# A hybrid decoder layer: turned blocks in a ring of five, and low parts of the gate/up operands on VectorE

## The chip, the cores and the metric

The kernel runs on one core of a Trainium2 chip. The core has a matrix engine (TensorE; PE in the profile, PEld for its weight loads), VectorE (DVE), ScalarE (ACT), GpSimd (POOL), SyncE (SP, which here only issues transfers), and 16 DMA engines. Each engine runs its own instructions in one fixed order and waits on semaphores for the others. The metric is the device time of one execution in microseconds; of several runs the median counts.

## The reference

One decoder layer on x of 2048 rows by 1024 columns, all float32:

```python
hn = rms_norm(h, mix_pre_g)
proj = hn @ w_in
attn_out = sliding_window_attention(q, k, v, attn_sinks, rel_bias)
conv_out = conformer_conv(u, conv_dw, conv_dw_b, conv_ln_g, conv_ln_b, w_conv_pw)
mixed = jnp.concatenate([attn_out, conv_out], axis=-1) @ w_out
h = h + rms_norm(mixed, mix_post_g)
hn = rms_norm(h, ffn_pre_g)
ff = (jax.nn.silu(hn @ w_gate) * (hn @ w_up)) @ w_down
h = h + rms_norm(ff, ffn_post_g)
```

The feed-forward width is 2816. The change touches the operands of `hn @ w_gate` and `hn @ w_up`.

## The kernel before

**Tiles.** The 2048 rows are four token tiles of 512 (`T`), numbered 0 to 3. A block is 128 partitions (`P`) by 512 columns, or 128 by 128 inside a transpose.

**High and low parts.** Every large float32 product is made of three faster ones. An operand x is split into a high part, which ScalarE writes by a copy into the reduced type float32r, and a low part, x minus the high part, which VectorE or GpSimd makes by a subtraction. `three` and `product` then add high by high, high by low and low by high into one PSUM bank. `split_f` makes the high part, `lo(x, w, on_pool)` the low part: on GpSimd if `on_pool` is true, otherwise on VectorE.

**Stages.** The letter before the @ of a label, or after it in the profile's names, tells the stage: A the input projection, B attention, C the convolution, J a join of two weight matrices, W the output projection with its norm, H the operands of gate and up, F gate and up, G the down projection and the last norm.

**Gate and up.** Stages H, F and G work on token tiles in pairs, first (0, 1), then (2, 3); `ws` holds the pair, so `ws[0]` is 0 or 2. Over a pair, gate and up are computed by a two-by-two block scheme with seven products instead of eight (`STEPS`); the weight blocks are A11 to A22 and their sums S1 to S4, the token blocks B11 to B22 and their sums T1 to T4. One product (`product`) is four blocks of 128 times three matmuls, 12 matmuls with 512 columns.

- `stage_h_plain` makes B11 or B21, the plain operands from the first tile of the pair: per block it loads columns of the normed rows, turns them on PE (`turned`) into a PSUM bank, copies them to a buffer `u` with the gain as scale, issues on ScalarE's queue a transfer that stores `u` in `hT`, and makes high and low part. For the first pair the turned blocks use the bank tag `ct`, of which there is one, and `u` the tag `gb`, of which there are two. The four blocks of B11 and the four of B21 make eight such copies. They run in the lane `lh` beside the output projection of tile 1 (`stage_w(1, ...)`), whose operands are named hl@W; attention on tile 3 runs there too.
- `stage_h_sums` makes T1 to T4 and B22, four blocks each; for T1, T3 and T4 the low part is made by GpSimd, for T2 by VectorE. It uses three tiles of tag `chl` per block, one of them for two blocks of `hT` read back.
- `stage_pre` runs the products of the first m with plain operands alone (A11 with B11, then A12 with B21), while the sums are made: 20 values of m in the first pair, 16 in the second, two products each. Its `split` makes the operands of the weights three products ahead. In the second pair the low parts of the odd ones, 16 in all, go to GpSimd.
- `stage_p1` runs the other products of the scheme. In the second pair it has GpSimd make some low parts of its own (`POOL_LO`) and the sums of finished blocks.

When the second pair's `stage_pre` runs, the last rows of the first pair's down projection are normed and stored beside it (`finish`, lane `lf`; names x@G, p@G, sm@G).

**Rings.** `t_(tag, ...)` takes the next buffer of a tag; `BUFS` says how many there are (`gb` 2, `chl` 5). A new tile waits until the tile that held the buffer last has been read for the last time, by a transfer too. A `chl` tile is two blocks wide.

**Order.** Lanes (`Lane`) are generators that are pumped as the main loop goes on, so the text order interleaves the stages. The framework then plans the order on each engine from that text order as a priority and its own estimate of times (`schedule_with_timeline_sim=True`), so that an instruction may be put ahead of others that were written before it.

Of the kernel before, what the change touches and what calls it, by code (L numbers as in the profile page):

```python
# [25 lines left out]
P = 128  # L26
T = 512
# [10 lines left out]
def layer_kernel(ctx, tc, x, xT, cols, rows, sinks, relb, onehot, w_in, w_pw, w_out, w_gate, w_up, w_down, out):  # L38
# [10 lines left out]
    def nm(s):  # L49
        uid[0] += 1  # L50
        return f"{s}@{lab[0]}_{uid[0]}"
# [3 lines left out]
    def t_(tag, shape, dt=F32):  # L55
        return sb.tile(list(shape), dt, tag=tag, name=nm(tag), bufs=BUFS[tag])
# [4 lines left out]
    def f2(tag, shape=(P, T)):  # L61
        return t_(tag, shape)

    def hl(tag):
        return t_(tag, (P, 2, T), F32R)
# [779 lines left out]
    def split_f(x, w):  # L845
        act(w[:, 0], x, AF.Copy)  # L846
        return w

    def lo(x, w, on_pool):
        (ptt if on_pool else vtt)(w[:, 1], x, w[:, 0].bitcast(F32), ALU.subtract)  # L850
# [9 lines left out]
    def turned(w, k, bank_of, tag):  # L860
        c = load_cols(w, k, tag)
        b = bank_of()
        for s in range(4):
            nc.tensor.transpose(b[:, s * P : (s + 1) * P], c[:, s], ident)
        return b

    def op_tile(ws, ops, n, k, spare):
        tag = OPTAG[ws[0]][n][k]
        if tag == "yt":
            if "yt" not in spare:  # L870
                spare["yt"] = t_("yt", (P, 2, 2, T), F32R)
            w = spare["yt"][:, k]
        else:
            w = hl(tag)
        ops.setdefault(n, []).append(w)
        return w

    def stage_h_plain(ws, ops, n, off):
        L = f"H{ws[0]}"
        for k in range(4):  # L880
            lab[0] = L
            b = turned(ws[0], k + off, tr if ws[0] else ct, COLTAG[ws[0]][k] if ws[0] else "fa")
            u = f2("gb")
            act(u, b, AF.Copy, scale=g_ffn[:, k + off : k + off + 1])
            nc.scalar.dma_start(hT[ws[0] // 2][k + off], u)
            o = op_tile(ws, ops, n, k, {})
            act(o[:, 0], u, AF.Copy)
            lo(u, o, False)
            yield 2.0

    def stage_h_sums(ws, ops):
        L = f"H{ws[0]}"
        spare = {}
        for k in range(4):
            lab[0] = L
            ct_ = COLTAG[ws[0]]
            g1, g2 = g_ffn[:, k : k + 1], g_ffn[:, k + 4 : k + 5]
            own = t_("chl", (P, 2, T))
            nc.sync.dma_start(own, hT[ws[0] // 2][k :: 4].rearrange("j p t -> p j t"))
            own = own[:, 0], own[:, 1]  # L900
            b12 = turned(ws[1], k, tr, ct_[2])
            b22 = turned(ws[1], k + 4, tr, ct_[3])
            r = t_("chl", (P, 2, T))
            t = t_("chl", (P, 2, T))
            act(r[:, 1], b12, AF.Copy, scale=g1)
            b = op_tile(ws, ops, "B22", k, spare)
            act(b[:, 0], b22, AF.Copy, scale=g2)
            yield 1.5
            lab[0] = L
            stt(r[:, 0], b12, g1, own[0], ALU.mult, ALU.subtract)  # L910
            stt(t[:, 0], b22, g2, r[:, 0], ALU.mult, ALU.subtract)
            stt(r[:, 1], b22, g2, r[:, 1], ALU.mult, ALU.subtract)
            stt(b[:, 1], b22, g2, b[:, 0].bitcast(F32), ALU.mult, ALU.subtract)
            vtt(t[:, 1], own[1], t[:, 0], ALU.subtract)
            yield 3
            for n, x in (("T1", r[:, 0]), ("T2", t[:, 0]), ("T3", r[:, 1]), ("T4", t[:, 1])):
                lab[0] = L
                o = op_tile(ws, ops, n, k, spare)
                act(o[:, 0], x, AF.Copy)
                lo(x, o, n != "T2")  # L920
                yield 0.8

    STEPS = [("A", "A11", "B11"), ("C", "S1", "T1"), ("B", "S2", "T2"), ("A", "A12", "B21"),
# [4 lines left out]
    def product(o, w, op, first):  # L928
        n = 0
        for k in range(4):  # L930
            ks = slice(k * P, (k + 1) * P)
            for a, b in ((0, 0), (0, 1), (1, 0)):
                mat(o, w[:, a, ks], op[k][:, b], start=first and n == 0, stop=n == 11, skip_group_check=not first)
                n += 1

    def stage_pre(ws, ops, mid, keep):
        PRE, two = PRES[ws[0]], TWO[ws[0]]
        L = f"F{ws[0]}"
        seq = [(m, half) for half in range(2) for m in range(two)]
        for m in range(two, PRE, 2):  # L940
            seq += [(m + j, half) for half in range(2) for j in range(2)]
        raws, wops, kept, seeded = {}, {}, {}, {}

        def load(q):
            if q < len(seq) and q % 2 == 0:
                lab[0] = L
                m, half = seq[q]
                raw = t_("raw", (P, 2, T))
                for j in range(2):
                    src, pr = MATS[m + j]  # L950
                    nc.sync.dma_start(raw[:, j], src[2 * pr][:, half * T : (half + 1) * T])
                    raws[q + j] = raw[:, j]

        def stored(q):
            return q == len(seq) or q < len(seq) and seq[q][1] and seq[q][0] < two

        def fetch(q):
            if stored(q):
                lab[0] = L
                kept[q] = f2("gb")  # L960
                nc.sync.dma_start(kept[q], keep[seq[q][0] if q < len(seq) else 0])

        def split(q):
            if q < len(seq):
                lab[0] = L
                raw = raws.pop(q)
                wops[q] = split_f(raw, hl("w"))
                lo(raw, wops[q], ws[0] and q % 2 == 1)

        def seed(q):  # L970
            if q < len(seq) and stored(q):
                lab[0] = L
                seeded[seq[q][0]] = mm()
                act(seeded[seq[q][0]], kept.pop(q), AF.Copy)

        load(0)
        load(2)
        for q in range(3):
            split(q)
        for q, (m, half) in enumerate(seq):  # L980
            started.add(f"P{ws[0]}.{q}")
            bn = "B21" if half else "B11"
            if len(ops.get(bn, ())) < 4:
                lh.until(f"{bn}.{ws[0]}")
            split(q + 3)
            load(q + 4)
            if stored(q + 2) and not stored(q + 1):
                fetch(q + 2)
            seed(q + 1)
            fetch(q + 3)  # L990
            lab[0] = L
            o = seeded.pop(m) if half else mm()
            product(o, wops.pop(q), ops[bn], not half)
            if not half:
                u = f2("fa")
                act(u, o, AF.Copy)
                nc.scalar.dma_start(keep[m], u)
                if m >= two:
                    seeded[m] = mm()
                    act(seeded[m], o, AF.Copy)  # L1000
            else:
                if MATS[m][0] is w_gate:
                    sg = f2("fa")
                    act(sg, o, AF.Silu)
                else:
                    vtt(sg, sg, o, ALU.mult)
                    nc.sync.dma_start(mid[0, MATS[m][1]], sg)
            yield 2.76
        early[ws[0]] = kept.pop(len(seq))
# [467 lines left out]
    ws, ops = (0, 1), {}  # L1477
    for n, off in (("B11", 0), ("B21", 4)):
        lh.add(n + ".0", stage_h_plain(ws, ops, n, off), lambda: since(lw, "W0", NH))
    run(stage_w(1, True, 2, "mid", "hl", "at", mm, norm=lambda g: lh.add("N1", g)))  # L1480
    lc.hold = lambda: "S0" not in lh.done
    lh.add("S0", stage_h_sums(ws, ops), lambda: f"P0.{PRE_S0}" in started and "B3" in lb.done)
    run(stage_pre(ws, ops, mids[0], keeps[0]))
    lt.add("TS", stage_tsums(td))
# [4 lines left out]
    ws, ops = (2, 3), {}  # L1489
    lw.add("C2", stage_tail(2))  # L1490
    lw.add("W2", stage_w(2, True, 2, "mid", "ql", "at", tr))
    lw.add("C3", stage_tail(3), lambda: since(lc, "T3", CS))
    lw.add("W3", stage_w(3, True, 2, "mid", "ql", "at", tr, norm=lambda g: lw.add("N3", g)))
    lw.add("B11.2", stage_h_plain(ws, ops, "B11", 0))
    run(stage_p2((0, 1), mids[0], td))
    lw.until("N3")
    lh.add("B21.2", stage_h_plain(ws, ops, "B21", 4), lambda: since(lw, "N3", NS))
    lh.add("S2", stage_h_sums(ws, ops), lambda: f"P2.{PRE_S2}" in started)
    run(stage_pre(ws, ops, mids[1], keeps[1]))
    lf.until("E0.3")  # L1500
# [65 lines left out]
```

## Time and profile before

| | |
|---|---|
| time, median of 3 runs | 1950.22 us (1946.52 to 1950.82) |
| time of the profiled execution | 1949.98 us |
| its span (first to last instruction) | 1948.3 us |
| PE busy | 1904.7 us (98%) |
| VectorE busy | 1487.6 us (76%) |
| ScalarE busy | 970.7 us (50%) |
| GpSimd busy | 287.3 us (15%) |

A row of a view names the line of the kernel (often that of a helper: all of VectorE's operations through `dve` have L85, all matmuls through `mat` L108, all high parts of F, G and H's sums their own lines, all low parts on GpSimd L850), the engine and operation, then what is written and read, `out<-in`, with the stage behind the @. Where such a row ends with square brackets, the engine stood idle for that time before it, and what released it is named. Groups give the count, the busy time and the mean duration in ns.

### The profile page before, as it was taken

Reading aid. Unit: us, or ns where it says so; the run is one execution under the profiler, and the core shown is the slowest. Engines: PE = TensorE matmul, PEld = TensorE weight load, DVE = VectorE, ACT = ScalarE, POOL = GpSimd, SP = SyncE. Lnnn points to the kernel's source line nnn. Section 1 sums busy time; section 2 is a strip of 40 time slices with the busy share of each in tenths; the row PEclk is TensorE's granted clock in tenths of the full one; section 3 lists DMA queues with packets and bytes.
Section 4 is the critical chain, followed back from the end, with each engine's and each line's share of the span. In section 5 each row is a group of like instructions: output and inputs, shape, how many; then the busy total and the mean of one; then the engine's idle time right before and its main releaser. Section 6 shows DMA issues by size and latency. Waiting matters only on the chain.

```text
span 1948.3 us, 26825 instructions
## 1 busy us (share of the span) xinstructions
PE 1904.7 (98%) x8730; PEld 1537.8 (79%) x8730; DVE 1487.6 (76%) x2707; ACT 970.7 (50%) x1910; POOL 287.3 (15%) x367
## 2 busy tenths in 40 slices
PE   8999999999999999999999999999999999999998
PEld 7877776777678878878878778887888888888886
DVE  5999999897875899888988665788566665455557
ACT  5455344657567533333445565575443433345443
POOL 5100000211012100000000020015232332311000
PEclk9999999999899999999999999999999999999999
DMA  8897746669768676877496788699544442375664
GB/s 311 272 324 235 239 155 198 196 217 340 226 224 279 221 249 221 283 249 243 133 320 224 243 282 294 219 337 315 199 157 163 162 157 98 130 248 186 215 192 154
DMA packets 229180, 443.55 MB, mean 228 GB/s; under 512 B 22920, under 2 KB 48688, under 8 KB 229040
## 3 DMA queue, kind: packets, MB, share of 16 engines
q1 hardware_dynamic: 207408, 406.19, 62.6%
q10 hardware_dynamic: 19392, 28.32, 4.0%
q0 software_dynamic: 2240, 7.34, 1.0%
q8 instruction: 68, 1.11, 0.2%
q14 instruction: 72, 0.59, 0.1%
HBM read 320.64 MB, written 121.12 MB: 227 GB/s over the span
## 4 chain that ended last, share of the span: by engine, by line
PE 72%; DMA 14%; DVE 9%; issue 2%; ACT 2%; POOL 1%; SPq 0%; DVEq 0%; ACTq 0%; POOLq 0%
PE mm@F L108 34%; PE mm@G L108 15%; PE mm@A L108 10%; PE mm@W L108 4%; PE tr@W L108 3%; PE tr@B L108 2%; DVE fc@C L85 2%; DMA raw@A<-w_in 1%; PE ct@J L108 1%; DMA td<-fc@G 1%; DMA mixT<-fc@C 1%; DMA fc@G<-w_down 1%; PE tr@B L514 1%; DVE w@F L85 1%; DVE sm@G L85 1%
## 5 line engine op out<-in xcount | busy, mean ns | idle before, releaser
L85 DVE SCALAR_TENSOR_TENSOR fc@C<-glu@C,colt,fc@C 128x512 f32<-128x512 f32 x480 | 354.1, 754 | 2.6
L108 PE MATMUL mm@F<-hl@H,w@F 128*128 128x512 f32 x1056 | 254.7, 389 | 0.0
L108 PEld LDWEIGHTS mm@F<-hl@H,w@F 128*128 128x128 f32 x1056 | 197.9, 188 | 41.1
L108 PE MATMUL mm@G<-hl@G,hl@G 128*128 128x512 f32 x924 | 224.5, 393 | 3.2 <-ACT hl@G L846 1.8
L108 PE MATMUL mm@A<-hl@A,w@A 128*128 128x512 f32 x840 | 204.1, 394 | 2.8 <-DVE hl@A L85 1.2
L108 PEld LDWEIGHTS mm@G<-hl@G,hl@G 128*128 128x128 f32 x924 | 171.4, 188 | 40.2 <-ACT hl@G L846 2.7
L846 ACT ACTIVATE w@F<-chl@F 128x512 fp32r<-128x512 f32 x220 | 135.2, 625 | 132.0 <-PE mm@F L108 121.5
L108 PE MATMUL mm@G<-w@G,hl@G 128*128 128x512 f32 x876 | 199.5, 389 | 0.0
L108 PEld LDWEIGHTS mm@G<-w@G,hl@G 128*128 128x128 f32 x876 | 164.4, 188 | 34.1
L108 PEld LDWEIGHTS mm@A<-hl@A,w@A 128*128 128x128 f32 x840 | 155.7, 188 | 40.9 <-DVE hl@A L85 3.0
L85 DVE TENSOR_TENSOR w@F<-chl@F,w@F 128x512 fp32r<-128x512 f32 x198 | 146.2, 741 | 31.9 <-ACT w@F L846 31.2
L108 PE MATMUL mm@F<-ql@H,w@F 128*128 128x512 f32 x528 | 130.5, 391 | 4.4 <-ACT w@F L846 2.7
L108 PE MATMUL mm@F<-p@H,w@F 128*128 128x512 f32 x528 | 130.8, 393 | 0.9 <-ACT at@F L1104 0.9
L108 PE MATMUL mm@F<-mid@H,w@F 128*128 128x512 f32 x528 | 130.7, 391 | 0.5 <-ACT mm@F L1000 0.4
L108 PE MATMUL mm@F<-x@H,w@F 128*128 128x512 f32 x528 | 128.4, 391 | 0.0
L108 PEld LDWEIGHTS mm@F<-ql@H,w@F 128*128 128x128 f32 x528 | 98.3, 188 | 26.7 <-ACT w@F L846 3.7
L108 PEld LDWEIGHTS mm@F<-p@H,w@F 128*128 128x128 f32 x528 | 100.0, 190 | 22.5 <-ACT at@F L1104 1.6
L108 PEld LDWEIGHTS mm@F<-mid@H,w@F 128*128 128x128 f32 x528 | 99.3, 188 | 22.3 <-ACT mm@F L1000 1.1
L108 PEld LDWEIGHTS mm@F<-x@H,w@F 128*128 128x128 f32 x528 | 98.6, 188 | 21.9 <-issue 0.8
L133 ACT ACTIVATE w@A<-raw@A 128x512 fp32r<-128x512 f32 x110 | 67.5, 626 | 81.2 <-PE mm@A L108 46.7
L85 DVE TENSOR_TENSOR w@G<-raw@G,w@G 128x512 fp32r<-128x512 f32 x73 | 50.8, 696 | 68.2 <-ACT w@G L846 62.1
L108 PE MATMUL mm@W<-w@W,hl@W 128*128 128x512 f32 x384 | 99.5, 406 | 1.8 <-ACT hl@W L754 1.4
(310 smaller groups left out, 3244.4 us busy)
## 6 DMA issues: line engine op xcount, KB each, us to landing
mids<-fa@F SPq DMA_DIRECT2D x154, 256.0 KB, 2.6
raw@A<-w_in SPq DMA_DIRECT2D x55, 512.0 KB, 4.9
w@A<-lo_in SPq DMA_DIRECT2D x84, 256.0 KB, 3.6
fc@G<-mids SPq DMA_DIRECT2D x77, 256.0 KB, 3.4
fa@G<-mids SPq DMA_DIRECT2D x75, 256.0 KB, 5.1
w@W<-lo_out SPq DMA_DIRECT2D x48, 256.0 KB, 5.6
chl@F<-w_gate SPq DMA_DIRECT2D x22, 512.0 KB, 4.1
raw@F<-w_gate SPq DMA_DIRECT2D x22, 512.0 KB, 3.7
```

Source lines behind the costliest of these rows:

```text
L85: r = op(*args, **kw)
L108: r = nc.tensor.matmul(*args, **kw)
L133: act(w[:, 0], raw, AF.Copy)
L514: nc.tensor.transpose(o[:, i * P : (i + 1) * P], pr[:, 4 * g + i], ident)
L846: act(w[:, 0], x, AF.Copy)
```

## The change

In `stage_h_plain` the turned blocks of the first pair (from tile 0) are copied into one half of a `chl` tile, a ring of five, instead of a `gb` tile, a ring of two; the second pair keeps `gb`. In `stage_h_sums` the low parts of T1, T3 and T4 are made by VectorE in both pairs (24 subtractions). In `stage_pre` the low parts of the odd weight operands of the second pair are made by VectorE (16 subtractions).

```diff
@@ stage_h_plain @@
             b = turned(ws[0], k + off, tr if ws[0] else ct, COLTAG[ws[0]][k] if ws[0] else "fa")
-            u = f2("gb")
+            u = f2("gb") if ws[0] else t_("chl", (P, 2, T))[:, 0]
             act(u, b, AF.Copy, scale=g_ffn[:, k + off : k + off + 1])
@@ stage_h_sums @@
                 act(o[:, 0], x, AF.Copy)
-                lo(x, o, n != "T2")
+                lo(x, o, False)
@@ stage_pre, split @@
                 wops[q] = split_f(raw, hl("w"))
-                lo(raw, wops[q], ws[0] and q % 2 == 1)
+                lo(raw, wops[q], False)
```

## The prediction

> **What bounds the kernel now.** I read the chain of waits first, then the busy time by stretch, then the three places the diff touches.
>
> ```profile
> PE 72%; DMA 14%; DVE 9%; issue 2%; ACT 2%; POOL 1%; SPq 0%; DVEq 0%; ACTq 0%; POOLq 0%
> ```
> ```profile
> 600.00:660.00 60.00, 60.00 (x282) 49.83 (x281) 43.37 (x59) 40.58 (x75) 16.83 (x12) 1.00 0.76 252
> ...
> 1348.00:1440.00 92.00, 91.83 (x405) 76.01 (x406) 54.60 (x70) 44.86 (x82) 29.48 (x20) 1.00 0.62 213
> ```
>
> The columns are the stretch and its length, then the busy time of PE, PEld, DVE, ACT and POOL, the granted clock, and the DMA share and rate. TensorE (PE) sets the end, and the sums for the first pair of tiles (600 to 660) lie beside a PE that never stops. So the change can only pay where PE has gaps. There are two such places: the end of the output projection of tile 1 (511 to 530), where the turned blocks go through the ring of two, and the first products of the second pair (1308 to 1349).
>
> **The change, part by part.**
>
> (a) **Turned blocks into the ring of five.** Eight copies change their buffer; count, engine and store stay the same. Removed is the wait of a copy for the store of the copy two before it. The timelines of ACT and of PE around the fifth block:
>
> ```profile
> 521.41 0.69 ACT L884 ACTIVATE gb@H<-ct@H,colt 128x512 f32<-128x512 f32 x1 [3.49 <-DMA hT<-gb@H]
> ```
> ```profile
> 518.12 1.60 PE L108 MATMUL tr@B<-kz,ql@A 64*128 64x256 f32 x12 [0.53 <-DVE sm@B L472]
> 519.66 1.11 PE L514 MATMUL tr@B<-ident,p@B 128*128 128x128 f32 x4
> 522.15 1.11 PE L864 MATMUL ct@H<-ident,fa@H 128*128 128x128 f32 x4 [1.38 <-ACT gb@H L884]
> 523.70 6.57 PE L108 MATMUL mm@W<-w@W,hl@W 128*128 128x512 f32 x18 [0.43 <-ACT hl@W L754]
> 530.11 0.60 PE L514 MATMUL tr@B<-ident,p@B 128*128 128x128 f32 x4
> ```
>
> ACT stood from 517.92 to 521.41 for a store. Behind that copy in its queue stood the two ACT operations that make hl@W, and PE waited for both: 1.38 us for the single ct bank, then 0.43 us for hl@W. With the ring of five ACT goes on at 517.92, so hl@W comes 3.49 us earlier, by 519.6 or so. PE is then the later one: its transposes end at 519.66 + 1.11 = 520.77, the four of the next block take 1.11 more, and the 18 matmuls begin at 521.9 instead of 523.70: **1.8 us**.
>
> The 18 take 6.57 us because the clock is low:
>
> ```profile
> 518.00:519.00 1.00, 0.88 (x8) 0.88 (x10) 1.00 (x4) 0.00 (x0) 0.00 (x0) 0.60 0.98 338
> ...
> 528.00:529.00 1.00, 1.00 (x5) 0.78 (x5) 0.00 (x0) 1.00 (x7) 0.00 (x0) 0.78 0.85 328
> ```
> ```profile
> 709.43 2.93 PE L108 MATMUL mm@F<-yt@H,w@F 128*128 128x512 f32 x6 [2.19 <-DVE gb@F L85]
> ```
> ```profile
> 712.00:714.00 2.00, 2.00 (x8) 1.60 (x8) 0.86 (x2) 0.56 (x2) 0.00 (x0) 0.81 1.04 402
> ```
>
> Means of 0.60 and 0.78 between full and half clock put the fall at 518.2 and the return at 528.44, 4.74 us after the stream began. In the other such place the stream began at 709.43 and a mean of 0.81 over 712 to 714 puts the return at 712.76, 3.33 us after it. If the clock returns 4.74 us after the new start too, all moves by 1.8 us. If it returns after 3.3 us (525.2), 3.3 us of matmuls at twice 0.227 us (405 matmuls in 91.83 us from 1348 to 1440) are 7.3 of the 18, the other 10.7 take 2.4 us, the last ends at 527.6 instead of 530.11, and **2.5 us** are saved. I take 2.5: the second place is also a stop followed by an unbroken stream, while the first had the 0.43 us wait and late low parts in it. Bounds: 0 (PE then waits for something else) to 5.8 (rival 1). The Trainium skill, in "TensorE: Matmul & The Clock Gate", section "What's actually happening", says that the clock is decided at the ends of a free-running window of 3.4 us; 518.2 to 528.44 is 10.24 us, three such windows, which agrees, and the boundary at 525.0 gives an estimate of 2.6 us here.
>
> What is late next: the score transposes of the last attention block, whose VectorE operations also moved up, so I see nothing. The slots of the ring of five that the copies take hold operands of stages that ended 200 us earlier. The loads of the sums come after the eighth copy in the ring; I cost them at nothing, since 60 us of first products cover them.
>
> (b) **Low parts of the sums, first pair:** 12 subtractions from POOL to DVE. At 0.685 us (row below) that is 8.2 us on a DVE busy for 43.37 of 60 us under a PE busy for all 60. Nothing, either way; without that cover the first product with a sum would be late by up to 8.2 us.
>
> (c) **Low parts of the sums and of the odd first-product weights, second pair:** 12 + 16 subtractions. PE has gaps only until 1349, so that stretch counts; first its windows and one such gap:
>
> ```profile
> 1320.00:1330.00 10.00, 9.26 (x42) 7.33 (x40) 9.93 (x23) 5.80 (x12) 3.31 (x3) 1.00 0.84 257
> 1330.00:1340.00 10.00, 8.62 (x40) 6.56 (x39) 9.63 (x19) 4.99 (x10) 7.78 (x4) 1.00 0.99 333
> 1340.00:1350.00 10.00, 9.57 (x42) 7.53 (x42) 8.09 (x11) 6.30 (x12) 2.96 (x3) 1.00 0.91 293
> ```
> ```profile
> 1325.33 3.01 PE L108 MATMUL mm@F<-ql@H,w@F 128*128 128x512 f32 x12 [0.74 <-DVE fa@F L85]
> ```
>
> PE stands for 0.74 + 1.38 + 0.43 = 2.55 us here, and DVE is full: the multiplication that frees a bank is late in its queue. Adding work to a full DVE ought to hurt. But its operations are stretched (groups from 1308 to 1349, POOL's first, then DVE's; then DVE rows from 1255 to 1350 as a measure):
>
> ```profile
> L850 POOL TENSOR_TENSOR w@F<-raw@F,w@F 128x512 fp32r<-128x512 f32 x6 | 9.3, 1549 | 10.2 <-ACT w@F L846 10.2
> L850 POOL TENSOR_TENSOR yt@H<-chl@H,yt@H 128x512 fp32r<-128x512 f32 x2 | 5.6, 2784 | 0.0
> L850 POOL TENSOR_TENSOR hl@H<-chl@H,hl@H 128x512 fp32r<-128x512 f32 x3 | 3.9, 1288 | 5.3 <-ACT hl@H L919 5.3
> L850 POOL TENSOR_TENSOR x@H<-chl@H,x@H 128x512 fp32r<-128x512 f32 x2 | 3.6, 1818 | 4.6 <-ACT x@H L919 4.6
> ```
> ```profile
> L85 DVE SCALAR_TENSOR_TENSOR chl@H<-tr@H,colt,chl@H 128x512 f32<-128x512 f32 x8 | 5.7, 744 | 2.3 <-ACT p@H L907 2.3
> L85 DVE TENSOR_TENSOR w@F<-raw@F,w@F 128x512 fp32r<-128x512 f32 x6 | 4.8, 793 | 0.2 <-ACT w@F L846 0.2
> L85 DVE SCALAR_TENSOR_TENSOR x@G<-x@G,sm@G,wx@G 128x512 f32<-128x512 f32 x5 | 4.7, 950 | 0.2 <-DMA wx@G<-h_scr 0.2
> L85 DVE SCALAR_TENSOR_TENSOR p@G<-p@G,sm@G,wx@G 128x512 f32<-128x512 f32 x4 | 4.0, 1000 | 0.0
> L85 DVE TENSOR_SCALAR sm@G<-sm@G 128x2 int32<-128x2 int32 x4 | 3.8, 958 | 0.1
> L85 DVE TENSOR_TENSOR sm@G<-sm@G 128x2 f32<-128x2 f32 x8 | 3.4, 434 | 0.1
> L85 DVE SCALAR_TENSOR_TENSOR sm@G<-sm@G,sm@G 128x2 f32<-128x2 f32 x12 | 3.0, 247 | 0.2
> ```
> ```profile
> L85 DVE TENSOR_TENSOR hl@G<-mb@G,hl@G 128x512 fp32r<-128x512 f32 x15 | 10.3, 685 | 1.1 <-ACT hl@G L846 1.1
> ...
> L85 DVE SCALAR_TENSOR_TENSOR sm@W<-sm@W,sm@W 128x4 f32<-128x4 f32 x6 | 0.9, 155 | 0.0
> L85 DVE SCALAR_TENSOR_TENSOR mid@W<-mid@W,sm@W,gb@W 128x512 f32<-128x512 f32 x1 | 0.7, 744 | 0.0
> L85 DVE TENSOR_TENSOR sm@W<-sm@W 128x4 f32<-128x4 f32 x3 | 0.5, 157 | 0.0
> L85 DVE TENSOR_SCALAR sm@W<-sm@W 128x4 int32<-128x4 int32 x2 | 0.3, 170 | 0.1
> ```
>
> An integer operation on two columns takes 958 ns where one on four columns took 170. Excess over the measure, in us: 6 x 0.108, 5 x 0.206, 4 x 0.256, 4 x 0.788, 8 x 0.277 and 12 x 0.092, together 9.1. Operations that read a PSUM bank (tr@H, 744 ns) show none. So DVE waits while POOL works on SBUF. The 13 POOL operations become 13 x 0.685 = 8.9 us of DVE work, and 9.1 us of waiting go: DVE has no more to do than before, rather less, since a small operation stuck for 1 us and the POOL result of 1.3 to 2.8 us are both gone from the chains. The Trainium skill, "GPSIMD Engine Reference", section "Key points", states such contention for VectorE instructions with two SBUF inputs or in a two-port mode; the rows agree. Bounds for PE: from 2.55 saved to 6.5 lost (rival 2). I take **1.6 us** saved, the 1.17 us and more that DVE's own lateness holds up and part of the rest. A waiting low part would hold DVE's queue for ACT's high part, as the even halves' low parts do already; the loads are not touched.
>
> **Sum:** 2.5 + 0 + 1.6 = 4.1 us off the profiled 1949.98 (span 1948.3, 1.7 around it), 1945.9. The median of the runs lies 0.2 above that execution, so **1946.1 us**.
>
> **Rivals.**
>
> 1. *The stop at 518 shrinks so far that the clock never falls.* Then what PE did from 518.2 to 530.11 takes, at full clock, 0.8 for the score group (1.60 at half), two sets of transposes at 0.60 and 18 x 0.227, 6.1 us: 5.8 saved instead of 2.5, **1942.8**. For it: the fall follows a stretch with little PE work. Against: ACT's wait starts at 517.92, when most of that stretch is over.
>
> 2. *DVE becomes the bound from 1308 to 1349* (the other side): the stretching has another cause than POOL and stays. Then 8.9 us come onto a DVE that had 0.07 + 0.37 + 1.91 = 2.35 us free from 1320 to 1350; 6.5 us go to the bank releases and PE, and a clock that falls once (3.33 us at half) adds 1.7. With (a) saved: **1955.8**. It decides as soon as less than 2.4 us of the 9.1 go. For it: DVE at 9.93 of 10. Against: the unstretched PSUM group.
>
> 3. *The turned blocks do not hold PE*: the order on the engines is planned anew, and PE meets a softmax result or its one ct bank instead. Only (c) counts: **1948.6**.
>
> **Chances.** Forecast 0.50, rival 1 0.14, rival 2 0.19, rival 3 0.17. About 0.2% (3.9 us, below 1946.3 or above 1954.1) is what this kernel's measurement can tell. The order of instructions is planned anew, so the forecast itself holds within one stall such as that of (a), 2.5 us: 1943.6 to 1948.6, six tenths of it below 1946.3. Faster: 0.30 + 0.14 + 0.05 of rival 3 = 0.49; slower: 0.19 and 0.02 of disorder; the rest 0.30. Range: from beyond rival 1 to rival 2, 1941 to 1956.
>
> **What would show it.** (a) right: no ACT idle for the store of hT near 518, the 18 matmuls from about 522, the clock back by 525. (c) right: DVE's operations on two columns back at some 160 ns, gaps of PE between 1320 and 1350 under 1.3 us. (b): PE still 60 of 60. Wrong, if DVE stands at full with operations unstretched while PE waits for fa@F, or if gaps appear where no edit lies.

## The result, and the profile after

| | before | after |
|---|---|---|
| median of 13 runs each | 1950.86 us | 1944.26 us |
| time of the profiled execution | 1949.98 us | 1939.64 us |
| its span | 1948.3 us | 1937.9 us |

The ratio after to before is 0.9972, with a 95% interval of 0.9961 to 0.9984: 6.6 us between the medians where 4.1 had been forecast. Measured again among the experiments below (run e4_all) it was 0.9955 (0.9940 to 0.9971). One of the 13 runs after took 2646.97 us at a granted clock of 0.67, and the ratio leaves it out. The forecast of 1946.1 us and its range held, but of the three steps behind it (b) was wrong and (a) right for a partly wrong reason; that the sum came so close is in part luck.

The page of the changed kernel, its busy times and its chain of waits:

```profile
PE 1898.4 (98%) x8730; PEld 1536.7 (79%) x8730; DVE 1487.0 (77%) x2747; ACT 970.7 (50%) x1910; POOL 228.2 (12%) x327
...
PE 73%; DVE 10%; DMA 10%; issue 2%; ACT 2%; POOL 2%; SPq 0%; DVEq 0%; ACTq 0%; POOLq 0%
```

GpSimd lost 59 us of work, as 40 subtractions left it. VectorE, which took them, is as busy as before (1487.6 us then): what it took over, it got back from operations that are shorter now. PE still sets the end.

**The turned blocks.** The same two windows as in the prediction, then PE's timeline and ScalarE's copies, all of the changed kernel:

```profile
518.00:519.00 1.00, 0.94 (x11) 0.70 (x11) 1.00 (x7) 1.00 (x4) 0.00 (x0) 1.00 0.94 246
528.00:529.00 1.00, 1.00 (x7) 0.82 (x6) 0.89 (x4) 1.00 (x4) 0.00 (x0) 1.00 0.54 94
600.00:660.00 60.00, 60.00 (x282) 49.88 (x282) 47.03 (x75) 38.91 (x72) 0.00 (x0) 1.00 0.71 237
```
```profile
516.01 0.66 PE L864 MATMUL ct@H<-ident,fa@H 128*128 128x128 f32 x4
516.43 1.64 PE L108 MATMUL mm@W<-w@W,hl@W 128*128 128x512 f32 x6
517.91 0.60 PE L864 MATMUL ct@H<-ident,fa@H 128*128 128x128 f32 x4
...
521.24 0.66 PE L514 MATMUL tr@B<-ident,p@B 128*128 128x128 f32 x4 [0.67 <-ACT p@B L515]
521.82 0.66 PE L864 MATMUL ct@H<-ident,fa@H 128*128 128x128 f32 x4
523.52 1.08 PE L108 MATMUL tr@B<-p@B,vd@B 128*64 128x512 f32 x4 [1.05 <-POOL p@B L517]
```
```profile
519.00 0.67 ACT L884 ACTIVATE chl@H<-ct@H,colt 128x512 f32<-128x512 f32 x1
519.70 0.33 ACTq L885 DMA_DIRECT2D hT<-chl@H  x1
...
521.08 0.68 ACT L884 ACTIVATE chl@H<-ct@H,colt 128x512 f32<-128x512 f32 x1
521.80 0.33 ACTq L885 DMA_DIRECT2D hT<-chl@H  x1
```

No copy waits for a store of `hT` any more: the one at 521.08 has no idle time before it. The granted clock is 1.00 where it was 0.60 and 0.78. PE does not run without stops, though. Matmuls of the output projection now stand between two turned blocks (516.43), where the order before had let them wait for the end, and PE's stops in these 20 us are for the softmax: 0.67 us for ScalarE and 1.05 us for GpSimd. The third window is the cover that step (b) relied on, and PE is busy in all of it.

At 590 us, where no edit lies, there is a stop that the kernel before does not have. PE's row, then two of ScalarE's, all of the changed kernel:

```profile
590.40 3.01 PE L108 MATMUL mm@F<-hl@H,w@F 128*128 128x512 f32 x12 [1.16 <-ACT mm@F L1000]
```
```profile
588.25 1.13 ACT L831 ACTIVATE mid@W<-mid@W,sm@W 128x1024 f32<-128x1024 f32 x1
...
589.77 0.58 ACT L1000 ACTIVATE mm@F<-mm@F 128x512 f32<-128x512 f32 x1
```

ScalarE's queue now has operations of the output norm (mid@W) right ahead of the copy that fills PE's next bank. All six profiles with the ring, here and below, have this stop, of 0.60 to 1.42 us, and none of the eight without it. Gaps where no edit lies were one of the prediction's signs of being wrong.

**The second pair's first products.** The stretch of 41 us that held PE's gaps, in the kernel before, then the same stretch of work after (7 us earlier):

```profile
1308.00:1349.00 41.00, 38.45 (x173) 30.34 (x172) 38.59 (x65) 27.31 (x56) 22.16 (x13) 1.00 0.92 297
```
```profile
1301.00:1342.00 41.00, 41.00 (x190) 33.83 (x189) 33.46 (x76) 26.90 (x56) 0.00 (x0) 1.00 0.93 307
```

PE's gaps went from 2.55 us to none. VectorE made 11 instructions more and yet was busy for 33.46 us instead of 38.59. Its groups in that stretch of the changed kernel say why:

```profile
L85 DVE TENSOR_TENSOR w@F<-raw@F,w@F 128x512 fp32r<-128x512 f32 x13 | 8.8, 687 | 1.0 <-ACT w@F L846 1.0
L85 DVE SCALAR_TENSOR_TENSOR x@G<-x@G,sm@G,wx@G 128x512 f32<-128x512 f32 x4 | 3.0, 750 | 3.2 <-DMA wx@G<-h_scr 3.2
L85 DVE SCALAR_TENSOR_TENSOR sm@G<-sm@G,sm@G 128x2 f32<-128x2 f32 x12 | 1.9, 156 | 0.1
L85 DVE TENSOR_TENSOR sm@G<-sm@G 128x2 f32<-128x2 f32 x8 | 1.2, 156 | 0.1
L85 DVE TENSOR_SCALAR sm@G<-sm@G 128x2 int32<-128x2 int32 x4 | 0.7, 166 | 0.0
```

Each line has its partner in the prediction: 793 ns became 687, 950 became 750, 247 and 434 both became 156, and 958 became 166. These are means; what they are made of is shown in the last section.

**A place without an edit.** From 656 us on, when the first pair's sums are done, PE begins the scheme's products, and no edit lies there. Still PE's window is fuller after the change; in the kernel before, then after:

```profile
656.00:716.00 60.00, 56.24 (x238) 45.14 (x237) 55.38 (x89) 22.20 (x41) 0.00 (x0) 0.97 0.76 249
```
```profile
656.00:716.00 60.00, 57.85 (x249) 47.38 (x248) 56.35 (x91) 22.56 (x41) 0.00 (x0) 0.97 0.77 249
```

PE's first stop in it before, then its only one after:

```profile
672.52 3.04 PE L108 MATMUL mm@F<-p@H,w@F 128*128 128x512 f32 x12 [0.85 <-ACT at@F L1104]
```
```profile
705.32 2.72 PE L108 MATMUL mm@F<-yt@H,w@F 128*128 128x512 f32 x6 [2.15 <-DVE gb@F L85]
```

The stop for ScalarE at 672 is gone, and so are two of 0.41 and 0.30 us. The one for VectorE's addition into gb@F, quoted at 709.43 in the prediction, is still there.

### The profile page after: what moved, and what is told of

Its sections match the earlier page's. It is cut to its first block, busy times and chain, and to the rows that moved or that the text cites. A ratio compares the mean times of both kernels' runs of the same rounds, so it can differ in the third digit from the quotient of the medians.

```text
span 1937.9 us, 26778 instructions
## 1 busy us (share of the span) xinstructions
PE 1898.4 (98%) x8730; PEld 1536.7 (79%) x8730; DVE 1487.0 (77%) x2747; ACT 970.7 (50%) x1910; POOL 228.2 (12%) x327
## 4 chain that ended last, share of the span: by engine, by line
PE 73%; DVE 10%; DMA 10%; issue 2%; ACT 2%; POOL 2%; SPq 0%; DVEq 0%; ACTq 0%; POOLq 0%
PE mm@F L108 35%; PE mm@G L108 18%; PE mm@A L108 7%; PE mm@W L108 4%; DVE fc@C L85 4%; PE tr@W L108 3%; PE tr@B L108 2%; DMA raw@A<-w_in 2%; PE ct@J L108 1%; DMA td<-fc@G 1%; DVE w@F L85 1%; PE tr@B L514 1%; DMA fc@G<-w_down 1%; DMA td<-wx@G 1%; DMA mids<-fa@F 1%
## 5 line engine op out<-in xcount | busy, mean ns | idle before, releaser
L108 PE MATMUL tr@W<-w@W,ql@W 128*128 128x512 f32 x384 | 96.9, 396 | 3.8 <-ACT ql@W L754 2.7
```

Of the source, the lines that this page charges most:

```text
L108: r = nc.tensor.matmul(*args, **kw)
```

## Where the time lies: three stretches of PE

To compare many kernels I cut each trace at starts of PE's matmuls, counted, so that the same products of a stage lie between two cuts in every kernel. The three stretches, in us:

- W: from the 193rd matmul of the output projection to the first of gate and up.
- P: from the 463rd to the 694th matmul of gate and up, in which the scheme's products begin (the 18 before them are still `stage_pre`). With no stop it takes 231 x 0.2267 = 52.4 us.
- S: from the 1849th to the 2311th, the second pair's first products.

| run | edit | W | P | S | ratio (95%) |
|---|---|---|---|---|---|
| before | none | 69.75 | 58.89 | 111.68 | |
| e8_before_again | none | 69.88 | 58.35 | 110.66 | 1.0002 (0.9987 to 1.0018) |
| e1_ring | (a) | 66.55 | 53.69 | 110.31 | 0.9979 (0.9966 to 0.9993) |
| e2_sums_first | (b) | 69.66 | 52.36 | 109.67 | 0.9955 (0.9938 to 0.9972) |
| e6_sums_first_again | (b) | 68.82 | 52.36 | 109.65 | 0.9962 (0.9948 to 0.9977) |
| e3_low_second | (c) | 70.13 | 57.51 | 109.41 | 0.9993 (0.9979 to 1.0006) |
| e5_two_of_three | 8 of the 12 of (b) | 69.36 | 55.39 | 108.97 | 0.9989 (0.9974 to 1.0003) |
| e7_more_on_gpsimd | (c) reversed | 69.40 | 58.41 | 113.37 | 1.0021 (1.0005 to 1.0037) |
| e9_pace | only another order | 69.76 | 55.59 | 113.15 | 1.0020 (1.0006 to 1.0034) |
| e10_ring_low_second | (a), (c) | 66.32 | 54.28 | 109.34 | 0.9969 (0.9954 to 0.9984) |
| e11_ring_sums_first | (a), (b) | 68.19 | 54.17 | 109.03 | 0.9965 (0.9948 to 0.9981) |
| after | (a), (b), (c) | 66.27 | 56.41 | 107.71 | 0.9972 (0.9961 to 0.9984) |
| e4_all | (a), (b), (c) | 65.56 | 55.71 | 107.71 | 0.9955 (0.9940 to 0.9971) |
| e12_whole_pace | all, another order | 66.59 | 52.44 | 109.49 | 0.9955 (0.9940 to 0.9971) |

A stretch is from one profiled execution, a ratio from 7 to 13 runs against the kernel before on the same chip. The executions of one kernel differ by some 0.3% either way, so one ratio has an interval of about 0.3%, 6 us, which is as much as the whole effect. The stretches tell more: in W and P the two executions of one kernel, where there are two, are at most 0.9 us apart (e11, below, shows some 2 us). The profiles of e3 and e9 are the slowest and the fastest of their 12 runs.

Two of the cuts are not quite like with like. In W the six kernels with the ring run 20 matmuls of attention (12 scores, eight transposes) more than the eight without, which run them after the cut; in S, e9 and e12 have eight transposes more than the others. At the 121st matmul of gate and up all fourteen kernels have run the same matmuls. From the start of W to there it takes 103.9 to 104.6 us without the ring, and with it 98.1 to 99.1 us in five profiles and 100.7 us in e11. So the ring is worth 5.0 us there on the mean, not the 3.0 us that W shows. The stop at 590 us takes 1.3 us of this back: to the 201st matmul, 3.7 us are left.

## The experiments

**e1_ring, e2_sums_first, e3_low_second, e4_all: each part alone, then all.** All diffs here are against the kernel before, unless another is named.

```diff
# e1_ring
-            u = f2("gb")
+            u = f2("gb") if ws[0] else t_("chl", (P, 2, T))[:, 0]
# e2_sums_first
-                lo(x, o, n != "T2")
+                lo(x, o, n != "T2" and ws[0])
# e3_low_second
-                lo(x, o, n != "T2")
+                lo(x, o, n != "T2" and not ws[0])
-                lo(raw, wops[q], ws[0] and q % 2 == 1)
+                lo(raw, wops[q], False)
# e4_all: the whole change
```

> The ring of five alone. Theory (each edit pays at its own place): the stretch from the first matmul of tile 1's output projection to the first matmul of gate and up, 69.8 us before and 66.3 us with the whole change, is 66 to 67 us; no half clock near 520; the gaps of PE in the second pair's first products (2.55 us before) stay; time 0.15 to 0.2% below before. Rival (the gain there comes from low parts or from chance): the stretch stays near 70 us, with half clock.

> Only the low parts of the first pair's sums on VectorE. Theory: nothing at their own place, since PE is full there; time within 0.1% of before. Rival: the 2.5 us that the whole change gained between 656 and 716 us (from the 463rd to the 694th matmul of gate and up) come from here; then this stretch is 56.5 us instead of 58.9 and the time 0.12% lower.

> Only the second pair's low parts (sums and odd weights) on VectorE. Theory (VectorE was held up by GpSimd): two-column operations on VectorE at 150 to 170 ns instead of 250 to 960, PE without gaps in the second pair's first products, the first 463 matmuls there in 107 to 108 us instead of 111.7; time 0.15 to 0.2% below before. Rival 2 of the prediction (VectorE becomes the bound): its operations stay stretched, PE loses up to 6.5 us more there, time 0.3% above.

> The whole change again, beside the parts and on their chip. If the edits add up, its time is the sum of the three: 0.3% below before, e1 and e3 each giving half. If the parts share one gain, it is no lower than the better of them.

Measured: 0.9979, 0.9955, 0.9993 and 0.9955. The surprise is the second. The edit that I had costed at nothing is alone worth as much as the whole, and it doesn't show under its own operations: PE was already full from 600 to 660. It shows in stretch P, where PE now has no stop at all (52.36). The ring too changed P (53.69) beside what it did in W, where it saved 3.3 us by this cut. e3 fell short of what was expected: S is 109.4 us instead of 107 to 108, with a stop of 1.27 us for fa@F left in it. And the parts do not add: 0.21 + 0.45 + 0.07 = 0.73% against 0.28 to 0.45% for the whole.

**e5_two_of_three, e6_sums_first_again, e9_pace: the work that moved, or the order?** The framework plans the order from its own estimate of times, so an edit at 610 us can change the order at 700 us. e5 moves 8 of the 12 subtractions, e6 repeats e2, and e9 moves none: it only paces the lane of the first pair's sums differently.

```diff
# e5_two_of_three
-                lo(x, o, n != "T2")
+                lo(x, o, n == "T4" or n in ("T1", "T3") and ws[0])
# e6_sums_first_again: as e2_sums_first
# e9_pace
-                yield 0.8
+                yield 0.6 if not ws[0] else 0.8
```

> First pair: the low parts of T1 and T3 on VectorE, T4 stays on GpSimd; 8 of the 12 subtractions of e2_sums_first. With these 8 the planned order of every engine is that of before but for the moved subtractions themselves and a few neighbours; with all 12 the order on PE, VectorE and the DMA queue is another one from about 690 us on. If moving the work is what pays in e2_sums_first (0.45% faster), this run has about two thirds of it, 0.3% faster. If the new order pays, this run is within 0.1% of before, and its PE has gaps in the scheme products of the first pair (656 to 980 us) like the one of before (6.4 us).

> The kernel of e2_sums_first once more. If its 0.45% is a property of its order, the ratio is 0.994 to 0.997 again, and PE's gaps from 656 to 980 us stay below 4 us (1.6 us in the first profile). If that was luck of seven runs, the ratio is near 0.999 and the gaps are 5 to 9 us as in the other profiles.

> The kernel before with the lane of the first pair's sums paced a little faster (yield 0.6 for 0.8): no instruction is added, removed or given to another engine, only the text order is another, and so the planned order. In the planned order VectorE's addition into gb@F stands right before the one into at@F in four of the first seven places of the scheme's products, where the kernel before has it behind at@F in each of the first four. If the gain of the first pair's low parts was the order: the stretch of PE from the scheme's first product to the 231st matmul after it (58.4 to 58.9 us in the kernel before, 52.4 in the kernel with the 12 low parts moved) falls to 52.4 to 56, ratio about 0.996 to 0.999 if the order is no worse elsewhere. If it was the GpSimd work itself: 58 to 59 again, ratio 1.000.

Ratios: 0.9989, 0.9962 and 1.0020. e6 agrees with e2, so that e2 was no luck. e5's ratio is the one expected if the order pays, yet its P has half of e2's gain (3.2 of 6.3 us). In the traces e5's matmuls and SP's transfers come in the same order as in the kernel before, from the first to the last, and on VectorE and ScalarE only the moved subtractions and a few neighbours differ. e6 has another order: its matmuls differ in eight places, all between 688 and 815 us of the kernel before.

The whole change has another order than before only ahead of the scheme's products (the last difference on PE lies at 630 us of the kernel before, 27 us before P begins) and again in the second pair. (a) and (b) each bring P a new order, and both together bring the old one back; so the parts need not add. All runs fall into four groups, by the engine of the first pair's low parts and by the order in P (stretch P in us):

| | order of before | another order |
|---|---|---|
| on GpSimd | 58.89, 58.35, 57.51, 58.41 (before, e8, e3, e7) | 53.69, 54.28, 55.59 (e1, e10, e9) |
| on VectorE (e5: 8 of 12) | 55.39, 54.17, 56.41, 55.71 (e5, e11, after, e4) | 52.36, 52.36, 52.44 (e2, e6, e12) |

The moved work shows in both columns, and the order in both rows. By the means, moving the work is worth 2.9 us with the order of before and 2.1 with others, and the other orders are worth 3.8 and 3.0 us. The orders in the right column are not all the same one, so its difference is the weaker evidence; the left column compares like with like. Its difference has some of the clock in it, though. In before, e8 and e7 a fall of 3.4 us at half clock lies in P, and in the lower field only in after. With a fall it is 58.55 us (mean of three) against 56.41, without one 57.51 (e3) against 55.09 (mean of three), so that the moved work is worth 2.1 and 2.4 us. In the right column e9 and e12 have the same order of matmuls in P: 55.59 and 52.44 us.

*What the moved work does.* VectorE's largest groups during the first pair's sums, 615 to 646 us in the kernel before, 613 to 644 after:

```profile
L85 DVE TENSOR_TENSOR w@F<-raw@F,w@F 128x512 fp32r<-128x512 f32 x9 | 9.8, 1084 | 0.2 <-ACT w@F L846 0.2
L85 DVE SCALAR_TENSOR_TENSOR chl@H<-tr@H,colt,chl@H 128x512 f32<-128x512 f32 x12 | 8.6, 745 | 2.6 <-ACT hl@H L907 1.3 <-POOL p@H L850 1.2
```
```profile
L85 DVE TENSOR_TENSOR w@F<-raw@F,w@F 128x512 fp32r<-128x512 f32 x10 | 6.9, 685 | 0.0
```

A low part takes 1084 ns beside GpSimd, 685 without it, and VectorE also stood 1.2 us for GpSimd's p@H: what the prediction saw in the second pair alone is here too. These low parts free the weights' buffers, for which SP's queue waits; SP in the kernel before, then after:

```profile
646.17 0.33 SPq L1027 DMA_DIRECT2D raw@F<-w_gate  x1
...
667.96 0.38 SPq L1059 DMA_DIRECT2D gb@F<-keeps  x1
```
```profile
641.91 0.33 SPq L1027 DMA_DIRECT2D raw@F<-w_gate  x1
...
663.91 0.38 SPq L1059 DMA_DIRECT2D gb@F<-keeps  x1
```

P begins at 657.00 before and at 655.41 after. Counted from there, these loads go out 2.7 and 2.5 us earlier. ScalarE waits for the second of them to seed a bank, before and after:

```profile
671.35 0.60 ACT L1090 ACTIVATE mm@F<-gb@F 128x512 f32<-128x512 f32 x1 [6.23 <-DMA gb@F<-keeps]
671.89 0.58 ACT L1104 ACTIVATE at@F<-mm@F 128x512 f32<-128x512 f32 x1
```
```profile
667.24 0.60 ACT L1090 ACTIVATE mm@F<-gb@F 128x512 f32<-128x512 f32 x1 [3.71 <-DMA gb@F<-keeps]
```

The copy into at@F behind it is what PE had waited for at 672.52. So the chain runs from GpSimd over VectorE and the weights' ring to SP's queue; from there three times to and fro between the loads of weights and VectorE's sums of them; and then over the load of gb@F and ScalarE to PE, 26 us behind the low parts. Its ends are in these rows. What a run tried is the first link alone, in the four runs of the lower left field. The stop at its end is there in before, e8, e3 and e7 (0.78 to 0.90 us) and in e9 (0.53), and in no profile with the low parts on VectorE; e1 and e10, in another order, do not have it either.

*What the order does.* VectorE's queue at the stop for gb@F, in the kernel before and in e6:

```profile
705.42 0.68 DVE L85 TENSOR_TENSOR at@F<-at@F,mm@F 128x512 f32<-128x512 f32 x1
...
708.69 0.68 DVE L85 TENSOR_TENSOR gb@F<-gb@F,mm@F 128x512 f32<-128x512 f32 x1
```
```profile
702.71 0.67 DVE L85 TENSOR_TENSOR gb@F<-gb@F,mm@F 128x512 f32<-128x512 f32 x1
...
704.57 0.67 DVE L85 TENSOR_TENSOR at@F<-at@F,mm@F 128x512 f32<-128x512 f32 x1
```

The addition into gb@F must have read a bank before the product with T4 (yt@H) may write into it; the one into at@F is in no such hurry. Where gb@F stands first PE has no stop, though VectorE is no less busy than before (55.38 us in the window above); the same window in e6:

```profile
656.00:716.00 60.00, 60.00 (x266) 49.67 (x266) 56.45 (x91) 24.78 (x44) 0.00 (x0) 1.00 0.75 245
```

In its planned order e9 has gb@F first in four of the first seven places, and P fell to 55.59 with no work moved. But e9 as a whole is slower, which I had not expected: PE's gaps from 656 to 985 add up to 8.1 us where before had 6.5, and S is 113.15, of which the eight transposes are about 1 us (an estimate: the changed kernel's S, without a stop, has 107.71 - 462 x 0.2267 = 3.0 us for 24). An order that is better in one place is not better as a whole.

**e7_more_on_gpsimd, e8_before_again: the dose of GpSimd.** The reverse of (c): all 32 low parts of the second pair's first-product weights go to GpSimd, so that VectorE has less to do. e8 is the kernel before, measured as a variant like any other.

```diff
# e7_more_on_gpsimd
-                lo(raw, wops[q], ws[0] and q % 2 == 1)
+                lo(raw, wops[q], ws[0])
# e8_before_again: no edit
```

> The second pair's first products with the low parts of all weight halves on GpSimd: 16 more than before go there. If VectorE is held up by GpSimd (theory), its operations are stretched more, although it has 16 x 0.685 = 11 us less to do: two-column operations keep a mean of 0.4 to 1 us, PE's first 463 matmuls of the second pair's gate and up take longer than the 111.7 us of before, 112 to 116. If VectorE's load is what matters (rival 2 of the prediction), they take less, 108 to 110 us.

> The kernel of before, unchanged, as a measure of what one profile and one comparison can tell: ratio 1 within its interval; stretches of its profile within about 1 us of the first profile, except the scheme products of the first pair (first pair's matmuls 463 to 1618, 273.7 us in the first profile), where I expect up to 5 us of difference.

e7 is slower by 0.2%, 1.0021, and e8 the same, 1.0002. The stretch in e7 by its window, by groups of VectorE and of GpSimd, and the stop that followed:

```profile
1304.00:1349.00 45.00, 41.80 (x188) 33.80 (x186) 39.34 (x60) 27.87 (x58) 30.28 (x23) 0.96 0.86 292
```
```profile
L85 DVE SCALAR_TENSOR_TENSOR chl@H<-tr@H,colt,chl@H 128x512 f32<-128x512 f32 x9 | 6.5, 746 | 2.7 <-ACT p@H L907 2.3 <-ACT chl@H L905 0.4
L85 DVE SCALAR_TENSOR_TENSOR sm@G<-sm@G,sm@G 128x2 f32<-128x2 f32 x12 | 5.2, 430 | 0.3
L85 DVE SCALAR_TENSOR_TENSOR x@G<-x@G,sm@G,wx@G 128x512 f32<-128x512 f32 x4 | 5.0, 1260 | 0.0
```
```profile
L850 POOL TENSOR_TENSOR w@F<-raw@F,w@F 128x512 fp32r<-128x512 f32 x12 | 17.6, 1478 | 5.9 <-ACT w@F L846 5.9
```
```profile
1326.85 4.43 PE L108 MATMUL mm@F<-ql@H,w@F 128*128 128x512 f32 x12 [2.98 <-DVE fa@F L85]
```

Six more subtractions are on GpSimd in that stretch (12 instead of 6). On the mean x@G is stretched further, to 1260 ns (950 before, 750 after), and so is the one kind of small operation in the groups, to 430 ns (247 before, 156 after). Those that read a PSUM bank still take 746. Not every kind is: over S, six small operations took more than 1.2 us in e7 and seven in the kernel before. In sum the effect is clear. Over S, beyond the usual duration of each operation (the 20th percentile of the 14 profiles), VectorE was held up for 20.1 us in e7, for 15.5 to 18.1 us in the seven others with before's order and low parts of this pair on GpSimd, and for 0.2 us in the five with (c). PE waits 2.98 us for the same multiplication as at 1325 in the kernel before, and the clock falls. VectorE with less work became later: the stretching is GpSimd's doing, and in sum it grows with GpSimd's work.

**e10_ring_low_second, e11_ring_sums_first, e12_whole_pace: pairs of parts, and another order for the whole.**

```diff
# e10_ring_low_second, against the whole change
-                lo(x, o, False)
+                lo(x, o, n != "T2" and not ws[0])
# e11_ring_sums_first, against the whole change
-                lo(x, o, False)
+                lo(x, o, n != "T2" and ws[0])
-                lo(raw, wops[q], False)
+                lo(raw, wops[q], ws[0] and q % 2 == 1)
# e12_whole_pace, against the whole change
-                yield 0.8
+                yield 0.6 if not ws[0] else 0.8
```

> The ring of five and the second pair's low parts on VectorE; the first pair's low parts of the sums stay on GpSimd, so the planned order of the scheme's first products is that of the ring alone. If each stretch keeps what it had where its edit stood alone: 66.5 us from the 193rd matmul of the output projection to the first of gate and up (69.4 to 70.1 without the ring), 53.7 us from the scheme's first product to the 231st matmul after it (58.4 to 58.9 before), 107.7 to 109.4 in the second pair's first products (110 to 111.7 before); together 3.3 + 4.9 + 2 = 10 us, ratio 0.995, as good as the whole change or 0.0005 better. If the edit of the first pair is needed for the gain: ratio 0.998, as with the ring alone.

> The ring and the first pair's low parts on VectorE, the second pair's on GpSimd as before: the whole change without its last part. Its planned order of the scheme's first products is the whole change's. If what matters is the planned order: 55.7 to 56.4 us for the scheme's first 231 matmuls, as in the whole change, not the 52.4 of the first pair's low parts alone; 66 us at the output projection; 110 to 111 us in the second pair's first products, 2 to 3 us more than the whole change. Ratio 0.9965 to 0.998. If the gain of each part stood by itself, 3.3 + 6.3 = 9.6 us, ratio 0.995.

> The whole change with the first pair's sums paced at 0.6: again only another planned order. VectorE's addition into gb@F stands before at@F in three of the first four places, against none of them in the whole change. If the order decides: the scheme's first 231 matmuls in 52.4 to 55 us instead of 55.7 to 56.4, ratio 0.993 to 0.996. If it doesn't: 56 us, ratio as the whole change, 0.9955 to 0.997.

e10: the stretches came as expected (66.32, 54.28, 109.34), but the ratio is 0.9969, not 0.995: the three sum to 9.7 us against the mean of before and e8, the medians show 7.7 (1943.00 against 1950.71), and the ratio 6. e11: 0.9965, as expected from the order; but W was 68.19 instead of 66 and P 54.17 instead of 56, although order and operations are the whole change's up to the second pair. So these stretches vary by some 2 us for one and the same program. In P the changed kernel has a fall of the clock and e11 none. W has a cause that can be seen as well; PE's timeline and windows of e11:

```profile
518.00 0.66 PE L514 MATMUL tr@B<-ident,p@B 128*128 128x128 f32 x4 [0.68 <-ACT p@B L515]
...
520.28 1.87 PE L108 MATMUL tr@B<-p@B,vd@B 128*64 128x512 f32 x4 [1.05 <-POOL p@B L517]
```
```profile
520.00:522.00 2.00, 1.72 (x6) 0.51 (x8) 1.97 (x11) 2.00 (x7) 0.23 (x1) 0.61 0.70 197
522.00:524.00 2.00, 2.00 (x8) 0.39 (x6) 0.72 (x2) 2.00 (x13) 0.00 (x0) 0.54 0.65 249
524.00:526.00 2.00, 2.00 (x18) 1.58 (x17) 1.19 (x4) 1.84 (x7) 0.00 (x0) 1.00 0.49 72
```

The stops are those of the changed kernel, 0.68 and 1.05 us at the same instructions, but here the clock fell. Half clock for (1 - 0.61) x 2 / 0.5 = 1.6 us and (1 - 0.54) x 2 / 0.5 = 1.8 us makes 3.4 us, and the 1.7 us that this costs is most of what W is longer by.

e12: stretch P fell to 52.44, as expected from the order, and its profile has the shortest span of all, 1935.7 us. The ratio, 0.9955, is that of e4 and lies where both expectations meet, so it doesn't tell them apart. S is 1.8 us longer than in the whole change, in another order, about 1 us of it for the eight transposes that this order brings into S.

No version beats the whole change by more than the intervals: the best four lie at 0.9955 to 0.9962, two of them with edit (b) alone.

## Why the prediction was right, and where it was not

**(a), the ring: right in cause, too small in size, wrong about the clock.** The forecast was 2.5 us. Over equal work, to the 121st matmul of gate and up, it takes 104.2 us on the mean of the eight profiles without the ring and 99.1 of the six with it: 5.0 us less, and 3.7 behind the stop at 590 us. ScalarE's idle time for the store of `hT`, 2.9 to 4.0 us in each of the eight, is gone in all six, as said. The step that failed is "the clock returns after 3.3 us", which took for granted that it still falls. In all eight profiles without the ring it does; in five of the six with it, it does not, which is rival 1's condition. These five gain 5.4 us, close to rival 1's price of 5.8, and e11, where it fell, 3.4. A second step failed beside it: for what is late next the prediction said "I see nothing", and PE met the softmax, part of what rival 3 had named, and the stop at 590 us. The two errors have opposite signs, so that the net gain is nearer to the forecast than its parts; that is luck. The order, too, was not the one that the timeline assumed: the 18 matmuls, expected from about 522, ran from 527.92 in the changed kernel, behind the softmax.

**(b), the first pair: wrong.** "Nothing, either way" holds for 600 to 660, where PE stayed full. The step that failed was to take that cover for the whole price: the subtractions were weighed against the PE above them, and not followed through the buffers and loads behind them to the first products after the cover's end. In the whole change P is shorter by 2.6 us (58.6 as the mean of before and e8, 56.1 of after and e4), of which 2.1 to 2.4 us are the moved work's with the clock's share taken out. The chain above ends in the stop of 0.85 us that is gone, and with it went two of 0.41 and 0.30 us; where the rest comes from is not shown. The rows were there: the stretch by GpSimd that the prediction found from 1308 on could have been looked for at 615, where nine low parts took 1084 ns each. With (b) alone the order changes too, and P is 6.3 us shorter. For that the prediction had allowed one stall of 2.5 us either way; in the whole change it did not happen in P.

**(c), the second pair: right in mechanism as far as it was tried, 1.4 to 1.6 us against 1.6.** Orders differ little between a kernel and the same with (c) added. S then changes from 111.2 (before and e8) to 109.4 in e3, from 110.3 (e1) to 109.3 in e10, and from 109.0 (e11) to 107.7 in after and e4: 1.8, 1.0 and 1.3. Without (c) the order of S is the same in before, e1, e2, e5, e6, e8 and e11, and its length still varies from 109.0 to 111.7. Much of that goes with (b), whose edit lies 600 us earlier (e7, e9 and e12 aside): without (c), S is 109.0 to 109.7 us in the four with (b) or most of it (e2, e6, e5, e11) and 110.3 to 111.7 in the three without; with (c) it is 107.7 with (b) and 109.3 to 109.4 (e3, e10) without. Between equals, then, (c) is worth 1.5 to 1.6 us and (b) as much again in S, for which no run shows the cause. e3's ratio, 0.9993 (0.9979 to 1.0006), agrees with 1.4 us but could not show it alone. What is shown is that GpSimd's work holds VectorE up: the small operations fell to 156 and 166 ns, and with e7 the stop for fa@F grew to 2.98 us, in before's order. That the holding by itself sets the length of S is not shown: in e5 and e11 VectorE was held for 16.7 and 15.5 us, against 18.1 in before, and S is 109.0 in both. Also, (c) gives PE another order at three places of S, and no run separates that from the moved work. Rival 2, VectorE as the bound, is refuted: the stretching went with GpSimd's work. Its condition had a slip, too: 8.9 us more against 2.35 free decides as soon as less than 6.5 us of the 9.1 go, not 2.4.

**Rivals and sum.** Against the mean of before and e8, the profiles of after and e4 are shorter by 3.9 us in W, 2.6 in P and 3.5 in S. Together these are 9.9 us, while their spans differ by 8.5, so that the rest of the program took 1.4 us more: there lie the stop at 590 us (1.2 us in these two) and the stretch after P, 1.9 us longer. The medians say 6.6 and 9.8. The forecast of 4.1 came out too small by the missing term (b) and by the size of (a).

**Open.** Where e9 loses again what P gained, and why e12's ratio is no better than e4's, is settled only in part. The stretch after P (from the 694th to the 1618th matmul of gate and up) takes 210 to 220 us in these profiles, with no pattern by edit, and is longer or shorter by more than the effects sought.

## What to carry to other kernels

An operation under a full PE is not free: follow the buffers that it frees to the loads that wait for them, and those to the first place where PE can stop. Before handing a busy VectorE's work to GpSimd, compare the durations of single VectorE operations with and without GpSimd beside them; here VectorE was less busy with the work than without. Where a framework plans the order, an edit can also re-plan it far away, so parts need not add: compare the programs' orders before reading a difference as the work's, and test the order with an edit that moves no work.

## What the runs showed of the hardware that was not expected

The same stops can cost a clock fall or none. The changed kernel stopped for 0.67 and 1.05 us (granted clock 1.00 at 518 and 528, above) and e11 for 0.68 and 1.05 us at the same instructions, with 3.4 us at half clock behind it. The clock records of the traces tell the two apart. Within one profile the falls lie whole multiples of 3.413 us apart: in e11 at 329.28, 520.43, 837.87 and 1001.71 us, 56, 93 and 48 such windows from one to the next. Cut into these windows, e11 has both stops in the one that ends at 520.43, and PE was busy for 49% of it. In the other five with the ring a boundary lies between the two stops or within the second, and no window there is below 64%. From 40 to 1920 us of all 14 profiles, each of the 48 falls came at the end of a window in which PE was busy for 10 to 55%, and no window of full clock below 45% passed without one. The Trainium skill, in "TensorE: Matmul & The Clock Gate", section "What's actually happening", says that the window of 3.4 us runs freely and that its phase makes the outcome vary from run to run; the trace agrees, with one such window of 3.4 us in e11. So the price of two stops of about 1 us here depends on whether they share a window: five times in six they did not.

VectorE's small operations are held until an operation of GpSimd ends, or not at all, and the means above mix the two. Two of one kind from the kernel before, then GpSimd's operation beside the first:

```profile
1313.09 1.28 DVE L85 TENSOR_TENSOR sm@G<-sm@G 128x2 f32<-128x2 f32 x1
...
1319.76 0.15 DVE L85 TENSOR_TENSOR sm@G<-sm@G 128x2 f32<-128x2 f32 x1
```
```profile
1312.53 1.82 POOL L850 TENSOR_TENSOR x@H<-chl@H,x@H 128x512 fp32r<-128x512 f32 x1 [2.44 <-ACT x@H L919]
```

The first ends with GpSimd's, at 1314.37 and 1314.35. Of the 26 operations on two columns in S of the kernel before, seven took 1.21 to 1.29 us and one 0.59, and each of these eight ended 0.02 to 0.03 us behind an operation of GpSimd; the other 18 took 0.15 to 0.16. So 958 ns says that three of four were held, and 247 that one of twelve was. Four of the seven name one tile as their source (TENSOR_SCALAR), so that "the rows agree" in the prediction is shown for operations with two SBUF sources; in what mode these four ran, no row tells.
